# Reciprocal roots as a power on GpSimd, and another order of the first experts' splits and of the output norm, in a hybrid decoder trunk

## The chip, the cores and the metric

The kernel runs on one core of one Trainium2 chip. The metric is the device time of one execution in microseconds (us), as the median of several runs; a separate execution was profiled. The engines are TensorE (PE, with its weight loads PEld), VectorE (DVE), ScalarE (ACT), GpSimd (POOL) and SyncE (SP). SP issues most DMAs; POOL issues the indirect ones (gathers and scatters by token index). Each engine works through its own instructions in order.

## The reference

The input is 1024 tokens of 1024 channels and a memory of 256 tokens. One layer is computed in float32, then a last norm:

```
h = rmsnorm(x, g_mix); x = x + gated_branch_mixer(h)       # conv 31, pool, short conv, gates
x = x + cross_attention(rmsnorm(x, g_x), rmsnorm(mem, g_mem))
t = rmsnorm(x, g_ffn)
p_grp = softmax(t @ w_rg + b_rg); pick 1 of 4 groups
p_exp = softmax of the 4 experts in the group; pick 2, weights renormalized, times the group's
x = x + sum over the 2 experts of weight * (silu(t @ w_gate) * (t @ w_up)) @ w_down
out = rmsnorm(x, g_f)
rmsnorm(x, g) = x * (mean(x * x) + 1e-6) ** -0.5 * g
```

Sixteen experts of width 256. Every norm needs, for each token, the reciprocal root of its mean square; the change is about how that root is computed and where the last norm's work stands.

## The kernel before, in words

**Layout.** Tokens lie on the 128 partitions, so there are 8 row tiles of 128 tokens x 1024 channels. Matrix products are done in three float32r passes: each operand is split into a high part (`wh`, a cast on ScalarE) and a remainder (`wl`, a subtraction on VectorE or GpSimd, line 117), and `mm3` (lines 60 to 64) multiplies high by high, high by low and low by high. `Stream` loads weights into raw buffers (`load_to`, line 93) and splits them (`split_to`, lines 112 to 117) ahead of their use; `units_of` says which engines split an item. For the experts' stream, item `EW + 6 e + q` is block q (4 of gate and up, 2 of down) of expert e in the order of work.

**Order.** The order of the instructions on every engine is that of the program (a manual schedule): the mixer's projections, then row-tile loops "w" (output projection), "s" (scores) and "v" (attention output), with helpers for the next tile's work put between the matmuls, then the experts.

**Roots.** `rstd_of` (line 166) turns sums of squares, which ScalarE accumulates with a Square activation, into reciprocal roots: `v = ss / D + eps` (line 174), a first guess by integer shift and subtraction (lines 175 and 176), `v = -v / 2` (line 177), and three Newton rounds of two instructions for one column (lines 180 and 181) or four for several (lines 183 to 186). The first three are always on VectorE, the rest on `unit`: VectorE, or GpSimd for the mixer's input norm (two roots of 4 columns, `prep_rstd`), for the last norm's tiles, and for one of the final blocks. It is called for the memory (2 columns), the mixer's input, the 8 row tiles of the norm ahead of attention (`w_norm`), the 8 ahead of the experts (`post_v`, and by hand for the last tile) and the last norm.

**The last row tile before routing** (from line 1067). Row tile 7 of "v" is done in halves. `add_half` adds the residual on VectorE (line 1080), squares on ScalarE (line 1081), and multiplies by the gain on GpSimd (line 1082). The root scales the normalized row (line 1107, stored for the gathers by a DMA from ScalarE's queue) and the logits of routing (line 897), from which the experts, ranks and token lists of all slots follow; then the first gathers go out (line 1153).

**The first experts.** After the gathers of experts 0 and 1 the weights 4 and 5 are split (`ast.split_to(EW + 6)`); VectorE works out the weights of the slots, TensorE transposes expert 0's rows (line 1182) and sums the slot weights (`pw`, line 1235), weight 6 is split, gate-up of expert 0 (line 1197) runs, `wslot` is written (lines 1243 to 1245), and weights 7 to 9 are split. GpSimd takes the remainders of weights 4, 5 and 7.

**The experts.** Each expert e has up to two blocks of 128 slots. Block 0: gate-up (`gu`), Silu times up (`act_of`, lines 1255 and 1256), transposes (`at`, line 1291), `down` (`y`); block 1 (`xb`, `gub`, `atb`, `yb`) runs under an If on the count of tokens. The results of experts 0 to 13 are scaled by the slot weight and scatter-added to `x2` in DRAM (line 1157).

**The last norm.** While experts 14 and 15 (`E1`, `E2`) compute, all 8 row tiles of `x2` are loaded (`norm_load`, line 1324), squared (1328), scaled (1336) and stored to `out` (1337), as if the last two experts had added nothing. Their tokens' rows are gathered (`rows_in`), get the expert's result (`final_add`, line 1351), squares (1352), a root (`final_rstd`, line 1354) and scaling (1361), and are scattered over the rows in `out` (`rows_out`, line 1345). The scatters write the same tensor as the stores and as one another, so each waits until those before it have landed. The dictionary `HOOKS` (line 1383) says at which place of which expert each of these steps is issued; expert 15 is (-1, ...). In this input expert 14 has one block, expert 15 two, and three scatters are issued: (E1, 0), (E2, 0), (E2, 1).

## Time and profile before

| what | value |
|---|---|
| runs | 1354.13 us median of 3 (1353.12 to 1354.61) |
| profiled execution | 1349.84 us |
| its span, first to last instruction | 1348.2 us |
| mean granted TensorE clock | 0.974 of full speed |
| busy: PE, DVE, ACT, POOL | 1268.7, 811.1, 447.6, 144.9 us |

Times in rows are in us from the span's start unless marked ns. `x8` is the number of instructions merged in a row; the bracket at a row's end is the idle time of the engine just before it and what released it. `SPq` and `POOLq` are the instruction queues of SP and POOL (DMA issue, waits), L1337 is line 1337 of the kernel. Busy shares are averages over stages with different limits; the waits and the chain say what ended last at a place.

### The profile page before, as it was taken

To read this page: it belongs to the slowest core of one execution; us is meant where nothing else is said; L and a number is where in the kernel's file an instruction comes from. 1 tells how busy PE (TensorE), PEld (TensorE's weight loads), DVE (VectorE), ACT (ScalarE), POOL (GpSimd) and SP (SyncE) were. 2 spreads that over 40 slices of the span, in tenths; PEclk is the share of its full clock that TensorE was granted. 3 is DMA by queue.
4 is the path that set the end of the run, shared out by engine and by line. 5 is a ranking of instruction groups with operands and counts; after the bars stand their busy time and mean duration, and the time that the engine had idled before them with its cause. 6 is when DMAs were issued, how large, how long until landed. Compare 5 with 4: busy or idle time off the path is not lost. (4 is left out here: it accounts for less than half of the span.)

```text
span 1348.2 us, 16066 instructions
## 1 busy us (share of the span) xinstructions
PE 1268.7 (94%) x6150; PEld 1054.2 (78%) x6151; DVE 811.1 (60%) x1210; ACT 447.6 (33%) x611; POOL 144.9 (11%) x157
## 2 busy tenths in 40 slices
PE   7999999999999999999999999999999689998871
PEld 7988888888888888888888898887888477776661
DVE  5836787887874356322344554335777767657665
ACT  6511221221111133212132253435312456555571
POOL 2400000000000000000000020011000423212243
PEclk8999999999999999999999999999999799999986
DMA  7641111121111112111153240113434788979773
GB/s 290 214 145 47 39 63 32 52 78 33 50 58 48 48 34 60 42 52 63 32 199 114 94 158 2 57 43 121 137 113 159 259 285 272 271 216 343 243 240 144
DMA packets 46490, 166.83 MB, mean 124 GB/s; under 512 B 5376, under 2 KB 6144, under 8 KB 46400
## 3 DMA queue, kind: packets, MB, share of 16 engines
q1 hardware_dynamic: 40032, 142.84, 30.8%
q0 software_dynamic: 6224, 22.29, 6.8%
q8 instruction: 54, 0.88, 0.3%
q10 hardware_dynamic: 144, 0.52, 0.1%
q14 instruction: 36, 0.29, 0.1%
HBM read 134.70 MB, written 30.93 MB: 123 GB/s over the span
## 5 line engine op out<-in xcount | busy, mean ns | idle before, releaser
L117 DVE TENSOR_TENSOR wl<-raw,wh 128x1024 fp32r<-128x1024 f32 (+1 forms) x179 | 213.5, 1228 | 145.7 <-ACT wh L114 145.6
L60 PE MATMUL ps<-hTh,wh 128*128 128x512 f32 x768 | 238.1, 390 | 0.0
L64 PE MATMUL ps<-hTh,wl 128*128 128x512 f32 x768 | 237.8, 389 | 0.0
L62 PE MATMUL ps<-hTl,wh 128*128 128x512 f32 x768 | 237.8, 389 | 0.0
L114 ACT CAST wh<-raw 128x1024 fp32r<-128x1024 f32 x197 | 194.8, 1036 | 97.0 <-PE ps L62 42.2
L60 PEld LDWEIGHTS ps<-hTh,wh 128*128 128x128 f32 x768 | 144.1, 188 | 30.4 <-issue 0.5
L64 PEld LDWEIGHTS ps<-hTh,wl 128*128 128x128 f32 x768 | 144.0, 188 | 30.2 <-DVE wl L117 0.2
L62 PEld LDWEIGHTS ps<-hTl,wh 128*128 128x128 f32 x768 | 144.1, 188 | 29.9
L431 DVE SCALAR_TENSOR_TENSOR conv<-glu,colt,conv 128x1024 f32<-128x1024 f32 x120 | 154.1, 1284 | 3.5
L117 POOL TENSOR_TENSOR wl<-raw,wh 128x1024 fp32r<-128x1024 f32 x18 | 44.2, 2461 | 235.3 <-ACT wh L114 235.3
L1157 POOL DMA_INDIRECT x_d<-merged,toki x20 | 37.9, 1897 | 154.2 <-DVE merged L1304 72.2
L60 PE MATMUL v<-Bh,aht 128*128 128x512 f32 x128 | 43.5, 411 | 0.0
L62 PE MATMUL v<-Bl,aht 128*128 128x512 f32 x128 | 41.0, 391 | 0.0
L64 PE MATMUL v<-Bh,alt 128*128 128x512 f32 x128 | 41.0, 391 | 0.0
L60 PE MATMUL s<-Ah,aht 128*128 128x512 f32 x128 | 40.1, 394 | 0.1
L60 PE MATMUL w<-wh,aht 128*128 128x512 f32 x128 | 40.0, 394 | 0.0
L64 PE MATMUL w<-wh,alt 128*128 128x512 f32 x128 | 39.6, 390 | 0.5 <-DVE alt L202 0.5
L64 PE MATMUL s<-Ah,alt 128*128 128x512 f32 x128 | 39.5, 390 | 0.0
L62 PE MATMUL s<-Al,aht 128*128 128x512 f32 x128 | 39.5, 389 | 0.0
L62 PE MATMUL w<-wl,aht 128*128 128x512 f32 x128 | 39.4, 389 | 0.0
L1197 PE MATMUL gu<-wh,xh 128*128 128x512 f32 x120 | 35.1, 415 | 4.0 <-DVE aTl L202 2.1
L1182 PE MATMUL xe<-ident,merged 128*128 128x128 f32 x128 | 18.9, 294 | 18.8 <-DMA merged<-t_d,toki 15.0
(434 smaller groups left out, 2136.0 us busy)
## 6 DMA issues: line engine op xcount, KB each, us to landing
raw<-in_w_e_dram SPq DMA_DIRECT2D x93, 512.0 KB
raw<-in_w_in_dram SPq DMA_DIRECT2D x48, 512.0 KB
raw<-in_w_kv_dram SPq DMA_DIRECT2D x16, 512.0 KB
x_d<-res SPq DMA_DIRECT2D x16, 512.0 KB
xr<-in_x_dram SPq DMA_DIRECT2D x8, 512.0 KB
raw<-in_w_ac_dram SPq DMA_DIRECT2D x8, 512.0 KB
raw<-in_w_o_dram SPq DMA_DIRECT2D x8, 512.0 KB
res<-in_x_dram SPq DMA_DIRECT2D x8, 512.0 KB
```

The costliest lines, as they stand in the source:

```text
L60: nc.tensor.matmul(o, lhsT=lhs.hi, rhs=r.hi, start=first, stop=False)
L62: nc.tensor.matmul(o, lhsT=lhs.hi, rhs=r.lo, start=False, stop=False)
L64: nc.tensor.matmul(o, lhsT=lhs.lo, rhs=r.hi, start=False, stop=last)
L114: e_hi.copy(hi, raw)
L117: e_lo.tensor_tensor(lo, raw, hi.bitcast(F32), op=OP.subtract)
L431: fillers.append(lambda k=k: dve.scalar_tensor_tensor(conv[i], glu[:, k:k + S], col("conv_w", i * TAPS + k), conv[i], op0=OP.mult, op1=OP. ...
L1157: pool_e.indirect_dma_start(out=x2_d[:, :], out_offset=bass.IndirectOffsetOnAxis(ap=idx, axis=0), in_=ys, in_offset=None, compute_op=OP.add)
L1182: pe.transpose(ps[k // 4][:, k % 4 * P:(k % 4 + 1) * P], src[:, k * P:(k + 1) * P], ident)
L1197: pe.matmul(ps, lhsT=getattr(xs[h], x)[:, k, :], rhs=getattr(w[2 * h + k // 2], y)[:, c0:c0 + 512], start=(h, k, x, y) == (0, 0, "hi", "hi ...
```

## The change

`rstd_of` becomes two GpSimd instructions: a multiply-add and a power with an exponent of -0.5 from a constant tile, which one memset fills at the start. All roots go there, with any number of columns; there is no Newton round left on any engine. For row tile 7 of "v" the first half's sum goes through a multiply-add on GpSimd as well, and the second half's product with the gain goes to VectorE. The split of weights 4 and 5 moves behind the slot-weight arithmetic, that of weight 6 behind `wslot`, which is now written ahead of gate-up of expert 0; the splits up to weight 9 and the loads stand ahead of gate-up. In the last norm the squares of the tiles move out of the end of expert 14 into expert 15, in pairs with a root each; the squares of the final blocks become a step of their own (`final_squares`), and the roots of expert 15's two blocks stand ahead of the second scatter on POOL.

```diff
--- before.py
+++ after.py
@@ -147,6 +147,8 @@
     sm = psums.enter_context(tc.tile_pool(name="sm", bufs=2, space=PSUM))
     small = ctx.enter_context(tc.tile_pool(name="small", bufs=2))
 
+    minus_half = small.tile([P, 2 * NT], F32, tag="mh", bufs=1, name="minus_half")
+
     def acc_tile(name):
         t = acc.tile([P, D], F32, tag="acc", name=name)
         return t
@@ -163,27 +165,13 @@
         c = CW[name] + i
         return colt[:, c:c + 1]
 
-    def rstd_of(ss, name, n=1, unit=None, y=None, base=EPS):
-        unit = unit or dve
+    def rstd_of(ss, name, n=1, y=None, base=EPS):
         pool = small if y is None else mo
         v = pool.tile([P, NT], F32, tag="v", bufs=2, name=f"v_{name}")[:, :n]
-        q = pool.tile([P, NT], F32, tag="q", bufs=2, name=f"q_{name}")[:, :n]
         if y is None:
             y = pool.tile([P, NT], F32, tag="y", bufs=2, name=f"y_{name}")[:, :n]
-        yi = y.bitcast(I32)
-        dve.tensor_scalar(v, ss, 1.0 / D, base, op0=OP.mult, op1=OP.add)
-        dve.tensor_scalar(yi, v.bitcast(I32), 1, None, op0=OP.logical_shift_right)
-        dve.tensor_scalar(yi, yi, -1, 0x5F3759DF, op0=OP.mult, op1=OP.add)
-        unit.tensor_scalar(v, v, -0.5, None, op0=OP.mult)
-        for _ in range(3):
-            if n == 1:
-                unit.tensor_scalar(q, y, v, y, op0=OP.mult, op1=OP.mult)
-                unit.tensor_scalar(y, q, 1.5, y, op0=OP.add, op1=OP.mult)
-            else:
-                unit.tensor_tensor(q, y, v, op=OP.mult)
-                unit.tensor_tensor(q, q, y, op=OP.mult)
-                unit.tensor_scalar(q, q, 1.5, None, op0=OP.add)
-                unit.tensor_tensor(y, q, y, op=OP.mult)
+        pool_e.tensor_scalar(v, ss, 1.0 / D, base, op0=OP.mult, op1=OP.add)
+        pool_e.tensor_tensor(y, v, minus_half[:, :n], op=OP.pow)
         return y
 
     def sumsq(src, junk, name):
@@ -238,6 +226,7 @@
     make_identity(nc, ident)
     dve.memset(onesm, 1.0 / 512)
     dve.memset(epst, EPS)
+    pool_e.memset(minus_half, -0.5)
     st.load_to(3)
     x_load(0)
     x_load(1)
@@ -255,7 +244,7 @@
         act.activation(junk, xr[key], AF.Square, accum_out=sums[b][:, i:i + 1])
 
     def prep_rstd(b, n):
-        rstds[b] = rstd_of(sums[b], b, n, unit=dve if b == "m" else pool_e)
+        rstds[b] = rstd_of(sums[b], b, n)
 
     def prep_scale(key, b, i, g):
         xn = pp.tile([P, D], F32, tag="xn", bufs=2, name=f"xn_{key}")
@@ -1079,7 +1068,7 @@
     def add_half(h):
         dve.tensor_tensor(x2[:, cols(h)], ph[h], x2[:, cols(h)], op=OP.add)
         act.activation(xn[:, cols(h)], x2[:, cols(h)], AF.Square, accum_out=(ss, ss2)[h])
-        pool_e.tensor_tensor(xgr[:, cols(h)], x2[:, cols(h)], grow[:, cols(h)], op=OP.mult)
+        (dve if h else pool_e).tensor_tensor(xgr[:, cols(h)], x2[:, cols(h)], grow[:, cols(h)], op=OP.mult)
 
     def tr_half(h):
         if not h:
@@ -1098,7 +1087,7 @@
     ast.load_to(EW + 2 * T7)
     add_half(1)
     nc.sync.dma_start(x2_d[T7 * P:, :][0:P, :], x2)
-    dve.tensor_scalar(ss, ss, 1.0 / D, EPS, op0=OP.mult, op1=OP.add)
+    pool_e.tensor_scalar(ss, ss, 1.0 / D, EPS, op0=OP.mult, op1=OP.add)
     rstd7 = rstd_of(ss2, "v7", base=ss)
     rt7 = sm.tile([P, 512], F32, tag="sm", name="rt7")
     logits(rt7, tT7, range(4))
@@ -1175,7 +1164,6 @@
 
     gather_both(0)
     gather_both(1)
-    ast.split_to(EW + 6)
 
     def x_tr(src, ps):
         for k in range(KD):
@@ -1219,6 +1207,7 @@
         dve.tensor_copy(wpart[:, :, :, c, :], wfull)
         if c < 2:
             dve.tensor_tensor(wfull, wfull, wpart[:, :, :, c, :], op=OP.subtract)
+    ast.split_to(EW + 6)
     xp = act_split("x0")
     xs0 = [xp[:, 4 * h:4 * h + 4, :] for h in range(2)]
     pxe = [acc_tile(f"xe0_{h}")[:, 0:512] for h in range(2)]
@@ -1236,13 +1225,14 @@
                           rhs=wpart[:, k, t].rearrange("p c e -> p (c e)"),
                           start=k == 0 and t == 0, stop=k == 1 and t == NT - 1)
     x_split(pxe, xs0)
-    ast.split_to(EW + 7)
-    w = [ast.get(EW + q) for q in range(6)]
-    gu0 = gate_up(xs0, w, acc_tile("gu0")[:, 0:512])
     pw3 = pw[:, 0:6 * NE].rearrange("p (b c e) -> p b c e", b=2, c=3)
     dve.tensor_copy(wslot, pw3[:, :, 0, :])
     dve.tensor_tensor(wslot, wslot, pw3[:, :, 1, :], op=OP.add)
     dve.tensor_tensor(wslot, wslot, pw3[:, :, 2, :], op=OP.add)
+    ast.split_to(EW + 10)
+    ast.load_to(EW + 18)
+    w = [ast.get(EW + q) for q in range(6)]
+    gu0 = gate_up(xs0, w, acc_tile("gu0")[:, 0:512])
     att.close()
     mo = ctx.enter_context(tc.tile_pool(name="mo", bufs=1, reuse_waits="tile"))
 
@@ -1257,10 +1247,11 @@
         return sg
 
     def gate_up_out(e, ps):
-        ast.split_to(EW + 6 * e + (8 if e else 10))
-        ast.load_to(EW + 6 * e + 23)
         if e == 0:
             gather_both(2)
+            return act_of(ps, f"{e}")
+        ast.split_to(EW + 6 * e + 8)
+        ast.load_to(EW + 6 * e + 23)
         return act_of(ps, f"{e}")
 
     def next_in(e, ps):
@@ -1268,6 +1259,7 @@
         x_in(xg[e + 1, 0], ps, xs)
         return xs
 
+    ast.load_to(EW + 23)
     sg = gate_up_out(0, gu0)
     xs1 = xs_tile("0b")
     xs0 = next_in(0, [sm.tile([P, 512], F32, tag="sm", name=f"xe1_{h}") for h in range(2)])
@@ -1328,7 +1320,7 @@
             act.activation(fjunk, nat[t], AF.Square, accum_out=nsum[:, t:t + 1])
 
     def norm_rstd(t0, t1):
-        rstd_of(nsum[:, t0:t1], f"n{t0}", t1 - t0, pool_e, nrstd[:, t0:t1])
+        rstd_of(nsum[:, t0:t1], f"n{t0}", t1 - t0, nrstd[:, t0:t1])
 
     def norm_scale(*ts):
         for t in ts:
@@ -1349,12 +1341,16 @@
         for h in range(2):
             f = fin[e, b][:, h * 512:(h + 1) * 512]
             dve.scalar_tensor_tensor(f, ps[h], w_of_slot(e, b), f, op0=OP.mult, op1=OP.add)
+
+    def final_squares(e, b):
+        for h in range(2):
+            f = fin[e, b][:, h * 512:(h + 1) * 512]
             act.activation(fjunk[:, 0:512], f, AF.Square, accum_out=fsum[:, e - NF, b, h:h + 1])
 
-    def final_rstd(e, b, unit):
+    def final_rstd(e, b):
         ss = fsum[:, e - NF, b]
-        dve.tensor_tensor(ss[:, 0:1], ss[:, 0:1], ss[:, 1:2], op=OP.add)
-        rstd_of(ss[:, 0:1], f"f{e}_{b}", 1, unit, frstd[:, e - NF, b:b + 1])
+        pool_e.tensor_scalar(ss[:, 0:1], ss[:, 0:1], 1.0 / D, EPS, op0=OP.mult, op1=OP.add)
+        rstd_of(ss[:, 1:2], f"f{e}_{b}", 1, frstd[:, e - NF, b:b + 1], base=ss[:, 0:1])
 
     def final_scale(e, b):
         f = fin[e, b]
@@ -1366,7 +1362,8 @@
         else:
             final_add(ps, e, b)
             if b and e < E2:
-                final_rstd(e, b, dve)
+                final_squares(e, b)
+                final_rstd(e, b)
                 final_scale(e, b)
 
     E1, E2 = NF, NE - 1
@@ -1381,12 +1378,13 @@
         rows_out(out, E1, 0)
 
     HOOKS = {
-        (-2, "end"): [lambda: norm_squares(0, 1, 2, 3), lambda: rows_in(E2, 0), lambda: norm_rstd(0, 4)],
-        (-1, "act"): [lambda: norm_squares(4)],
-        (-1, "put"): [lambda: norm_squares(5, 6, 7), lambda: norm_scale(0, 1, 2), lambda: norm_rstd(4, 8), lambda: norm_scale(3)],
-        (-1, "gate"): [lambda: final_rstd(E1, 0, pool_e)],
-        (-1, "act1"): [lambda: norm_scale(4, 5, 6, 7), lambda: final_scale(E1, 0), first_rows_out],
-        (-1, "put0"): [lambda: final_rstd(E2, 0, dve)],
+        (-2, "end"): [lambda: rows_in(E2, 0)],
+        (-1, "act"): [lambda: norm_squares(0, 1), lambda: norm_rstd(0, 2), lambda: norm_squares(2, 3), lambda: norm_rstd(2, 4)],
+        (-1, "put"): [lambda: norm_scale(0, 1, 2), lambda: norm_squares(4)],
+        (-1, "gate"): [lambda: norm_squares(5), lambda: norm_rstd(4, 6), lambda: norm_scale(3), lambda: norm_squares(6)],
+        (-1, "act1"): [lambda: norm_squares(7), lambda: norm_rstd(6, 8), lambda: final_squares(E1, 0), lambda: final_rstd(E1, 0),
+                       lambda: norm_scale(4, 5, 6, 7), lambda: final_scale(E1, 0), first_rows_out],
+        (-1, "put0"): [lambda: final_squares(E2, 0), lambda: final_rstd(E2, 0)],
         (-1, "late"): [lambda: final_scale(E2, 0), lambda: rows_out(out, E2, 0)],
     }
 
@@ -1445,8 +1443,9 @@
             down(yp1, aT1, w, 1)
             put(yp1, e, 1)
             if end:
+                final_squares(e, 1)
+                final_rstd(e, 1)
                 hook(e, "late")
-                final_rstd(e, 1, dve)
                 final_scale(e, 1)
                 rows_out(out, e, 1)
         with cmp.Else():
```

## Rows read from the trace of the kernel before

**Rows 1.** The page, busy time, share of the span and instructions of TensorE.

```profile
PE 1268.7 (94%) x6150; PEld 1054.2 (78%) x6151; DVE 811.1 (60%) x1210; ACT 447.6 (33%) x611; POOL 144.9 (11%) x157
```

**Rows 2.** Waits of TensorE over the span: in total, times, longest (us).

```profile
PE xe L1182 <- DMA merged<-t_d,toki: 15.0, 6, 4.4
```

**Rows 3.** Timeline of the start: start us, us, engine, line, operation, [idle].

```profile
42.44 0.23 POOL L177 TENSOR_SCALAR v<-v 128x4 f32<-128x4 f32 x1 [0.32 <-DVE y L175]
...
45.01 1.22 DVE L117 TENSOR_TENSOR wl<-raw,wh 128x1024 fp32r<-128x1024 f32 x1
...
47.11 2.39 POOL L117 TENSOR_TENSOR wl<-raw,wh 128x1024 fp32r<-128x1024 f32 x1
...
47.19 3.39 DVE L262 SCALAR_TENSOR_TENSOR xn<-xr,y,g_mix 128x1024 f32<-128x1024 f32 x1 [0.96 <-POOL y L186]
...
50.73 1.06 PE L197 MATMUL tr<-ident,xn 128*128 128x128 f32 x8 [1.27 <-DVE xn L262]
```

**Rows 4.** Timeline around the last row tile before routing.

```profile
1043.02 1.27 POOL L1082 TENSOR_TENSOR merged<-res,grow 128x512 f32<-128x512 f32 x1 [2.75 <-DVE ss_v7a L1101]
...
1043.57 0.19 ACT L1081 ACTIVATION_READ_ACCUMULATOR xnv<-res 128x1 f32 x1
...
1044.33 1.07 PE L889 MATMUL rt<-w_rt,merged 128*128 128x20 f32 x8 [0.49 <-ACT merged L1089]
...
1046.23 0.24 DVE L897 SCALAR_TENSOR_TENSOR lg<-rt,y_v,b_rt 128x20 f32<-128x20 f32 x1
```

**Rows 5.** Timeline around the first experts.

```profile
1057.87 7.12 POOL L117 TENSOR_TENSOR wl<-raw,wh 128x1024 fp32r<-128x1024 f32 x3
...
1059.99 6.09 DVE L117 TENSOR_TENSOR wl<-raw,wh 128x1024 fp32r<-128x1024 f32 x1
...
1066.01 0.18 DVE L1243 COPY wslot<-pw 128x32 f32<-128x32 f32 x1
...
1066.78 0.63 PE L1182 MATMUL xe<-ident,merged 128*128 128x128 f32 x4 [1.64 <-DVE wslot L1245]
...
1070.58 0.66 PE L1291 MATMUL at<-ident,sg 128*128 128x128 f32 x2 [3.17 <-DVE xl L202]
```

**Rows 6.** Timeline of the last expert.

```profile
1300.69 1.07 PE L1197 MATMUL gu<-wh,xl 128*128 128x512 f32 x4
...
1305.54 0.36 ACT L1255 ACTIVATE sg<-gu 128x256 f32<-128x256 f32 x1
...
1306.71 0.41 PE L1291 MATMUL at<-ident,sg 128*128 128x128 f32 x2 [3.37 <-DVE sg L1256]
...
1314.86 0.23 POOL L177 TENSOR_SCALAR v_n<-v_n 128x4 f32<-128x4 f32 x1 [1.64 <-DVE nrstd L175]
...
1318.03 0.42 DVE L202 TENSOR_TENSOR aTlb<-atb,aThb 128x256 fp32r<-128x256 f32 x1 [0.90 <-ACT aThb L201]
...
1319.41 4.89 DVE L1336 SCALAR_TENSOR_TENSOR nat<-nat,nrstd,grow 128x1024 f32<-128x1024 f32 x4 [0.96 <-POOL nrstd L186]
```

**Rows 7.** The same timeline, small instructions of GpSimd.

```profile
1306.13 0.24 POOL L177 TENSOR_SCALAR v_n<-v_n 128x4 f32<-128x4 f32 x1 [6.16 <-DVE nrstd L175]
...
1306.45 0.20 POOL L183 TENSOR_TENSOR q_n<-nrstd,v_n 128x4 f32<-128x4 f32 x1
...
1319.67 2.27 POOL L180 TENSOR_SCALAR q_f<-frstd,v_f 128x1 f32<-128x1 f32 x1
...
1325.42 0.27 POOL L181 TENSOR_SCALAR frstd<-q_f,frstd 128x1 f32<-128x1 f32 x1
```

**Rows 8.** The chain of waits at the end: start us, us, what.

```profile
1327.86 0.08 POOLq L1379
...
1329.17 3.45 DMA out_dram<-merged,toki
...
1334.50 3.33 DMA out_dram<-merged,toki
...
1338.59 0.90 POOL out_dram L1345
```

## The prediction

> **What bounds the kernel now.** I read the page first, then TensorE's waits, then the timeline around the places that the diff touches, and last the chain of waits. On the page the reader is to see that TensorE is busy for 94% of the span [rows 1]: an edit pays only where TensorE stands still, or behind its last matmul. The list of TensorE's waits says where it stands still [rows 2]: mostly behind gathers of tokens, which the diff leaves alone, and once, near 50 us, behind a normalized row tile, which needs a root [rows 3]. The four timelines that follow are the places touched: the start [rows 3], the last row tile before routing [rows 4], the first experts [rows 5] and the last expert with the output norm [rows 6]. The chain shows the end of the span, where TensorE has nothing left to do: three scatters into the output, one behind the other [rows 8].
>
> **Price of a root.** Before, a root is four instructions and three Newton rounds; after, it is a multiply-add and a power, both on GpSimd (the final ones two multiply-adds and a power). GpSimd's small multiply-add takes 0.24 us, a small product of two tiles 0.20 us, one with a scalar from a tile 0.27 us, and about 0.08 us lie between two of them [rows 7]. The trace has no power. Ends: 0.2 us, as the plain product, and 2.4 us, which GpSimd takes for a difference over 1024 columns [rows 3]; a function in place of a product on so few columns should lie near the small row, and I take **0.6 us** (an estimate: three times that row). A root is then 0.24 + 0.08 + 0.6 = 0.9 us, a final one 0.9 + 0.35 = 1.3 us.
>
> **The start.** GpSimd's root of row tiles 4 to 7 works from 42.44 until the weight remainder queued behind it starts at 47.11; VectorE's scaling of tile 4, in the same two microseconds, takes 3.39 us, and TensorE waits 1.27 us for it [rows 3]. With the root done by 43.4 the remainder moves some 2.5 us ahead, still next to VectorE's own remainder (45.01), which may then wait until about 47.0; scaling follows at 48.2 and ends at 49.5, where TensorE came free (50.73 - 1.27 = 49.46). I take **-1.0 us**; ends 0 and -1.3. The memory's root, that of tiles 0 to 3, the 8 of the next norm and the first 7 of the third go at nothing: their users are transposes and logits behind the matmuls of the following tile, and no other wait of TensorE names a root; VectorE's freed time lies under TensorE's matmuls too. GpSimd's weight remainders stand ahead of at most one such root, 2.4 us [rows 3]; without that cover it would be this much per root. The added memset of 16 columns lies ahead of GpSimd's first remainder, which waits for a weight.
>
> **The last row tile before routing.** ScalarE's sum of the second half is there at 1043.76, VectorE's ten instructions follow, and the logits' scaling on VectorE starts at 1046.23, while TensorE's last logits were done at 1044.33 + 1.07 = 1045.40 [rows 4]. After: GpSimd, idle for the 2.75 us before 1043.02 [rows 4], has its first multiply-add behind it; the second starts at 1043.85, and 0.27 + 0.08 + 0.6 put the root at 1044.8. The logits come last now: 1045.5, **-0.7 us**, until a power of 1.2 us. The second half's product with the gain (1.27 us on GpSimd [rows 4]) goes to VectorE, which has the 2.4 us of its root free there. The row's store leaves earlier too; the gather waits for the slots, not for it.
>
> **The first experts.** VectorE's remainder of weight 6 stands from 1059.99 to 1066.08, released only when GpSimd's three remainders end at 1064.99; the slot weights follow, and then two remainders [rows 5]. After, the three slot instructions (from 1066.01, some 0.2 us each) come first, at a time when VectorE would stand still anyway: **-0.6 us** for TensorE's transposes at 1070.58, which wait 3.17 us for the end of this queue. The second half of the next expert's transposes loses its wait of 1.64 us [rows 5], but the queue named ends last, so no more is counted. The splits of weights 4 and 5 move behind three small activations on ScalarE; GpSimd takes them only after its gathers at 1057.87, so nothing, and if ScalarE were late, the lateness. SP issues the same loads in the same order, POOL the same gathers.
>
> **The last expert.** gate-up ends at 1301.76, but ScalarE's Silu starts at 1305.54, behind squares of four row tiles that wait for their loads, and the transposes wait 3.37 us, until 1306.71 [rows 6]. After, Silu precedes the squares: the transposes go when the three matmuls ahead of them end, near 1303.3, **3.4 us** earlier, and all that follows on TensorE with them. VectorE's remainder of the second block (1318.03 to 1318.45) ends near 1315.05. Then come the last four scalings, which start at 1319.41 now since GpSimd's second Newton (from 1314.86) holds them [rows 6]. After, the pairs' roots are ready except the last: tile 7's square follows ScalarE's cast, some 3.4 us earlier too, at 1314.6 to 1315.85, the multiply-add is held by two scalings until 1317.7, the power ends at 1318.4. Scalings 4 and 5 from 1315.1, 6 and 7 from 1318.5 to 1320.95, against 1324.30: **-3.3 us** for the last store. The gather of expert 15's second block now stands ahead of the roots on POOL, not between them.
>
> **The scatters.** The first waits until POOL's queue moves on at 1327.86, when the stores have landed, and starts 1.31 us later; the second starts 5.33 us after it, the third 4.09 us after that [rows 8]. Landing takes 3.45 us, and from landing to the next start the third shows 0.76 us, so 4.2 us is the least. The 5.33 contain VectorE's Newton, sum and scaling. After, the roots of expert 15 stand on POOL behind the first scatter, the new wait: 0.9 us for issuing a scatter [rows 8], two roots of 1.3 us, and 0.8 us of gaps and semaphores, as from landing to start, give 4.3 us: **-1.0 us**. The final roots queue ahead of the second scatter, and whoever waits for them is VectorE's scaling and, through it, the third scatter, which keeps its 4.1 us.
>
> **Sum.** -1.0 - 0.7 - 0.6 - 3.3 - 1.0 = **-6.6 us**. The profiled execution took 1349.84 us (1348.2 of them its span), so 1343.2; it lies 4.3 us under the median of the runs, from which I take the same: **1347.5 us**. A power of 0.2 us gives 0.7 us more (1346.8). From 1.2 us on each further microsecond costs four: one before routing, one ahead of the last stores, two between scatters. With power c the change is 4c - 9.6, so 2.4 us gives 0 and 1354.1.
>
> **A rule weighed.** VectorE's stream of scalings holds GpSimd: the first scalar product takes 2.27 us next to it and one of the same kind after its end 0.27 us [rows 7]. The Trainium skill (SBUF — State Buffer, section Who interferes with whom) has it that a VectorE instruction with two inputs in SBUF and a GpSimd instruction that reads SBUF exclude each other, and that who issues first keeps the port for the whole instruction. By that rule the last pair's multiply-add waits for one scaling, and the sum gains some 0.2 us; the row shows that two can pass, which I used.
>
> **Rivals.**
> - *A slow power* (the other side). It sits in the queue of POOL between the scatters, twice, and before routing, once. For it: the trace has no such instruction, and VectorE's Newton, 1043.76 to 1046.23, was cheap [rows 4]. Against: the small rows there lie under 0.3 us when undisturbed [rows 7]. From 3.1 us it is slower by more than 0.2%; at 4 us, 4 x 4 - 9.6 = +6.4, **1360.5**. Chance 0.07; a power of 1.7 to 3.1 us, within 0.2%, 0.05.
> - *The experts swallow what comes before them.* For it: TensorE waits 15.0 us for gathers there [rows 2], which share DMA with the weights. Against: gathers and loads are released by work that itself comes earlier. Then only the tail's 4.3 us are left: **1349.8**. Chance 0.10.
> - *The port lock holds the paired roots.* Four roots of two instructions are strewn among eight scalings; at 2.27 us each instruction the last pairs come some 4 us later, the gain ahead of the stores goes, and about 2.6 us remain: **1351.5**. Against: VectorE stops when a root is missing, and then GpSimd runs. Chance 0.08.
> - *Forecast:* 0.70.
>
> **Numbers.** A measurement here can tell about 0.2% (2.7 us). Faster: 0.70 + 0.10 = 0.80; same: 0.08 + 0.05 = 0.13; slower 0.07. The range goes from 1344.8 (power 0.2 us, the whole 1.64 us of the transposes' wait, and the runs' spread of 0.8 us) to 1352.0, over the two rivals that are faster or even; what is left out is the slow power and a little below.
>
> **What would show it.** Each power near 0.6 us on GpSimd; no wait of TensorE's transposes near 49.5; the logits' scaling bound by TensorE; slot weights ahead of the remainder; Silu of expert 15 right behind gate-up; the last store some 3 us sooner against the experts' end; scatters 4.3 and 4.1 us apart. It is wrong if the power takes over 1.2 us, if the roots between the scatters set their distance, or if the last expert starts as late as before.

## The result and the profile after

The runs gave 1342.74 us for the kernel after (median of 5, 1339.88 to 1345.01) and 1354.13 us for the kernel before (median of 5, 1351.45 to 1356.98): a ratio of **0.9921 [0.9900, 0.9942]**, or -11.4 us between the medians. Predicted were 1347.5 us (range 1344.8 to 1352.0) and -6.6 us. The direction was right, the time lies below the range. The profiled execution after took 1344.64 us, with a span of 1342.9 us, so the two profiles differ by only 5.3 us of span. Which of these numbers is the change's is the first question that the experiments answer. Two executions of the kernel before beside later runs took 2587 and 3282 us; they are in no number here.

The page after, its line of busy times, answers to [rows 1]: TensorE has the same work, VectorE has lost 41 us and 214 instructions, most of them of the Newton rounds.

```profile
PE 1268.5 (94%) x6150; PEld 1055.0 (79%) x6151; DVE 770.4 (57%) x996; ACT 447.2 (33%) x611; POOL 147.1 (11%) x154
```

The start, in the timeline of after, answers to [rows 3] (start us, us, engine, line, operation, idle time before it).

```profile
40.55 1.01 POOL L174 TENSOR_TENSOR y<-v,minus_half 128x4 f32<-128x4 f32 x1
...
42.87 2.42 POOL L117 TENSOR_TENSOR wl<-raw,wh 128x1024 fp32r<-128x1024 f32 x1 [1.31 <-ACT wh L114]
43.20 3.16 DVE L117 TENSOR_TENSOR wl<-raw,wh 128x1024 fp32r<-128x1024 f32 x1
...
46.42 0.39 PE L64 MATMUL kv<-memTh,wl 128*128 128x256 f32 x1 [1.07 <-DVE wl L117]
```

A power of four columns takes 1.01 us. TensorE no longer waits for the scaled row tile. GpSimd's remainder now runs against VectorE's instead (43.20: 3.16 us for what takes 1.2 alone), and TensorE waits 1.07 us for that.

Row tile 7 and the first gather, same view, answer to [rows 4].

```profile
1041.69 0.27 POOL L173 TENSOR_SCALAR v_v<-ss_v7b,ss_v7a 128x1 f32<-128x1 f32 x1 [3.36 <-ACT xnv L1070]
1042.04 0.55 POOL L174 TENSOR_TENSOR y_v<-v_v,minus_half 128x1 f32<-128x1 f32 x1
1042.08 1.07 PE L878 MATMUL rt<-w_rt,merged 128*128 128x20 f32 x8 [0.49 <-ACT merged L1078]
...
1043.27 0.24 DVE L886 SCALAR_TENSOR_TENSOR lg<-rt,y_v,b_rt 128x20 f32<-128x20 f32 x1 [1.45 <-PE rk L904]
...
1043.80 0.35 ACTq L1097 DMA_DIRECT2D t_d<-xnv  x1
...
1049.21 0.19 DVE L933 TENSOR_TENSOR toki<-idxf,pi 128x32 int32<-128x32 f32 x1 [0.40 <-PE pc L1109]
...
1050.77 1.24 POOL L1142 DMA_INDIRECT merged<-t_d,toki  x1 [8.19 <-DVE gv L1201]
```

One column takes 0.55 us, and the logits' scaling (1043.27) now stands right behind TensorE's last logits (1042.08 + 1.07), as forecast. But the gather starts 1.56 us behind the token list (`toki`). In the profile that the prediction read it was 0.49 us:

```profile
1047.41 0.35 ACTq L1108 DMA_DIRECT2D t_d<-xnv  x1
...
1052.17 0.19 DVE L944 TENSOR_TENSOR toki<-idxf,pi 128x32 int32<-128x32 f32 x1 [0.40 <-PE pc L1120]
...
1052.66 1.21 POOL L1153 DMA_INDIRECT merged<-t_d,toki  x1 [8.37 <-DVE cntf L1167]
```

The first experts answer to [rows 5].

```profile
1055.50 7.09 POOL L117 TENSOR_TENSOR wl<-raw,wh 128x1024 fp32r<-128x1024 f32 x3
...
1058.65 0.19 DVE L1229 COPY wslot<-pw 128x32 f32<-128x32 f32 x1
...
1059.20 4.48 DVE L117 TENSOR_TENSOR wl<-raw,wh 128x1024 fp32r<-128x1024 f32 x1
...
1067.63 0.41 PE L1283 MATMUL at<-ident,sg 128*128 128x128 f32 x2 [2.55 <-DVE xl L190]
```

The last expert and the scatters answer to [rows 6 to 8].

```profile
1300.58 0.39 ACT L1245 ACTIVATE sg<-gu 128x256 f32<-128x256 f32 x1 [4.95 <-PE gu L1185]
...
1301.94 0.38 PE L1283 MATMUL at<-ident,sg 128*128 128x128 f32 x2
...
1306.10 2.48 DVE L1328 SCALAR_TENSOR_TENSOR nat<-nat,nrstd,grow 128x1024 f32<-128x1024 f32 x2 [0.90 <-POOL nrstd L174]
...
1307.42 1.21 POOL L173 TENSOR_SCALAR v_n<-nsum 128x2 f32<-128x2 f32 x1 [1.36 <-ACT fjunk L1320]
...
1316.63 2.48 DVE L1328 SCALAR_TENSOR_TENSOR nat<-nat,nrstd,grow 128x1024 f32<-128x1024 f32 x2 [0.58 <-POOL nrstd L174]
1316.68 1.28 POOL L1352 TENSOR_SCALAR fsum<-fsum 128x1 f32<-128x1 f32 x1
...
1319.33 0.56 POOL L174 TENSOR_TENSOR frstd<-v_f,minus_half 128x1 f32<-128x1 f32 x1
...
1322.84 1.07 POOL L1337 DMA_INDIRECT out_dram<-merged,toki  x1 [2.95 <-DVE merged L1343]
...
1325.27 1.28 POOL L1352 TENSOR_SCALAR fsum<-fsum 128x1 f32<-128x1 f32 x1
...
1327.59 1.28 DVE L1357 SCALAR_TENSOR_TENSOR merged<-merged,frstd,grow 128x1024 f32<-128x1024 f32 x1 [1.08 <-POOL frstd L174]
1327.74 2.07 POOL L1337 DMA_INDIRECT out_dram<-merged,toki  x1 [0.19 <-issue]
1333.36 0.90 POOL L1337 DMA_INDIRECT out_dram<-merged,toki  x1 [3.55 <-DMA out_dram<-merged,toki]
```

Silu stands right behind gate-up and the transposes wait for nothing. The scatters are 4.90 and 5.62 us apart, where 4.3 and 4.1 were forecast: the issue of the second one took 2.07 us next to a scaling on VectorE (1.07 us for the first), and the third waits for its landing.

### The profile page after: what moved, and what is told of

It is laid out like the page before. It is cut to its first block, busy times and chain, and to the rows that moved or that the text cites. A ratio compares the mean times of both kernels' runs of the same rounds, so it can differ in the third digit from the quotient of the medians.

```text
span 1342.9 us, 15878 instructions
## 1 busy us (share of the span) xinstructions
PE 1268.5 (94%) x6150; PEld 1055.0 (79%) x6151; DVE 770.4 (57%) x996; ACT 447.2 (33%) x611; POOL 147.1 (11%) x154
## 5 line engine op out<-in xcount | busy, mean ns | idle before, releaser
L117 DVE TENSOR_TENSOR wl<-raw,wh 128x1024 fp32r<-128x1024 f32 (+1 forms) x179 | 213.9, 1230 | 152.9 <-ACT wh L114 152.8
L1146 POOL DMA_INDIRECT x_d<-merged,toki x20 | 34.9, 1745 | 158.8 <-DVE merged L1296 57.1
L190 DVE TENSOR_TENSOR alt<-merged,aht 128x1024 fp32r<-128x1024 f32 (+1 forms) x25 | 30.4, 1221 | 13.1 <-ACT aht L189 13.1
```

The lines of the kernel that those rows point to most:

```text
L117: e_lo.tensor_tensor(lo, raw, hi.bitcast(F32), op=OP.subtract)
L190: dve.tensor_tensor(dst.lo, src, dst.hi.bitcast(F32), op=OP.subtract)
L1146: pool_e.indirect_dma_start(out=x2_d[:, :], out_offset=bass.IndirectOffsetOnAxis(ap=idx, axis=0), in_=ys, in_offset=None, compute_op=OP.add)
```

## The experiments

A term is small beside the differences between executions, so each experiment is read twice: in its ratio, and in the time between landmarks of its trace.

**The two kernels again.** No edit.

> The kernel before, unchanged, to see how far its executions lie apart and in what. Theory A (the profiled execution of before was a fast draw): single times spread over some 7 us, the median stays near 1353 to 1354, and the ratio to before is 1.000; the trace of a slow draw shows its extra microseconds in the experts' stage, as more time at the lower granted clock or longer waits for gathers. Theory B (the two profiles are typical and the change is worth the 5.2 us between them): executions lie within 1 us of 1350 when they share a chip with the others of this group.

Measured: 1352.85 us (1350.39 to 1359.17, 12 runs), ratio 0.9997 [0.9981, 1.0014], span 1353.4 us.

> The changed kernel, unchanged, beside the one before on one chip. Theory A: ratio 0.990 to 0.994 (10 us less), although the two profiles differ by 5.2 us alone. Theory B: ratio 0.996 (5 us less).

Measured: 1344.81 us (1343.09 to 1347.72, 6 runs), ratio 0.9937 [0.9919, 0.9955], span 1346.1 us.

> The kernel after, unchanged. Theory A (true change about -9 us, the mean over its executions so far): ratio 0.9925 to 0.994. Theory B (the -6.6 us of the prediction was right and the first sets were draws): ratio 0.995.

Measured, on another chip: 1343.59 us (1342.52 to 1345.38, 6 runs), ratio 0.9924 [0.9906, 0.9943], span 1341.3 us.

Theory A holds in the times; where a long execution loses its time is looked at below. All executions of before, 86 of them, have a mean of 1353.1 us and a standard deviation of 2.4; the profiled one, 1349.84, has 7 below it. The 17 executions of after have a mean of 1343.9. The change is worth **-9.1 us**, with some 0.5 us for the standard error of the two means.

**Parts of the change.** First the roots alone, with the experts' order and the norm's order of before:

```diff
-        dve.tensor_scalar(v, ss, 1.0 / D, base, op0=OP.mult, op1=OP.add)
...
-                unit.tensor_tensor(y, q, y, op=OP.mult)
+        pool_e.tensor_scalar(v, ss, 1.0 / D, base, op0=OP.mult, op1=OP.add)
+        pool_e.tensor_tensor(y, v, minus_half[:, :n], op=OP.pow)
```

> All roots by power on GpSimd, and row tile 7's sum and product as in the change, but the first experts and the last norm in the order of before. By the steps of the prediction and the trace of after: start -1.6, later row tiles -0.7, routing -0.7, and in the last norm GpSimd's second root takes 1.9 instead of 4.5 us and the final roots no longer hold VectorE, -2 to -4: -5 to -7 us in all (ratio 0.995 to 0.996). Rival: nearly the whole gain is in the roots, then -9 us or more (ratio under 0.9935); other rival: without the new order of the squares the tail gains nothing, then -3 us (0.998).

Measured: 1349.48 us (1344.9 to 1352.9, 11 runs), ratio 0.9970 [0.9954, 0.9987]; -4.2 us between the means. The end of the kernel did not gain (from the first load of the norm's rows to the third scatter 43.2 us, before 43.0 and 44.3).

Then the kernel after without the change's second part (splits, loads and `wslot` stand as before):

```diff
     x_split(pxe, xs0)
+    ast.split_to(EW + 7)
+    w = [ast.get(EW + q) for q in range(6)]
+    gu0 = gate_up(xs0, w, acc_tile("gu0")[:, 0:512])
     pw3 = pw[:, 0:6 * NE].rearrange("p (b c e) -> p b c e", b=2, c=3)
...
-    ast.split_to(EW + 10)
-    ast.load_to(EW + 18)
-    w = [ast.get(EW + q) for q in range(6)]
-    gu0 = gate_up(xs0, w, acc_tile("gu0")[:, 0:512])
...
```

> The change without its second part: splits 4 to 6 and the slot weights as before, roots and last norm as after. By the prediction's step the part is worth 0.6 us: time as after within 1 us, at most 1 us more. Rival (the experts' order carries what the prediction missed, by keeping TensorE's clock or by earlier gathers): 3 us or more above after.

Measured: 1342.83 us (1339.81 to 1345.99, 6 runs), ratio 0.9924 [0.9904, 0.9944]. It is not slower than after on the same chip (1344.81), so the rival falls. And the same part alone, on the kernel before (the diff of the change, from `ast.split_to(EW + 6)` to `ast.load_to(EW + 23)`):

> The kernel before with the second part of the change alone (splits 6 to 10 and the slot weights in the other order), Newton roots and the last norm as before. Theory A (the prediction's term, and what the profiles with and without it show at that place): first expert's first transposes to its gated products' transposes 12.2 to 12.6 us in place of 12.8 to 13.3, total -0.6 us, ratio 0.9985 to 1.001, not to be told from no change. Theory B (the later splits and loads cost something further on, as the 1 us between the kernels with and without this part suggests): ratio 1.0005 to 1.002.

Measured: 1353.74 us (1351.32 to 1356.70, 12 runs), ratio 1.0005 [0.9991, 1.0020]. From the token list to expert 0's `at` transposes it takes 17.83 us where four profiles with the old order and Newton roots show 18.4: -0.57 us at its place, nothing that can be told in the total. Theory A.

Then the last norm. Only the first four squares behind Silu, all roots by Newton:

```diff
-        (-2, "end"): [lambda: norm_squares(0, 1, 2, 3), lambda: rows_in(E2, 0), lambda: norm_rstd(0, 4)],
-        (-1, "act"): [lambda: norm_squares(4)],
+        (-2, "end"): [lambda: rows_in(E2, 0)],
+        (-1, "act"): [lambda: norm_squares(0, 1, 2, 3), lambda: norm_rstd(0, 4), lambda: norm_squares(4)],
```

> The kernel before with one thing of the last norm moved: the squares of row tiles 0 to 3 and their root stand behind the last expert's Silu, roots by Newton's steps as before. Theory A (the step of the prediction, 3.4 us on PE): the wait of the last expert's transposes for the gated products (3.4 to 4.9 us before) falls under 1 us, the last scatter lies 2 to 3.4 us earlier counted from the first load of the norm's rows (43.0 and 44.3 in the two profiles of before, so 40 to 42), ratio 0.9975 to 0.9985. Theory B (PE gains it, but the Newton root of the four tiles now comes late and the scalings wait for it): same short PE wait, but the scatters stand where they stood, ratio 0.9995 to 1.0005.

Measured: 1353.71 us (1349.00 to 1356.77, 12 runs), ratio 1.0003 [0.9988, 1.0018]. Theory B, to the letter; the timeline of this kernel shows it.

```profile
1306.10 0.39 ACT L1255 ACTIVATE sg<-gu 128x256 f32<-128x256 f32 x1 [5.17 <-PE gu L1197]
...
1307.49 0.38 PE L1291 MATMUL at<-ident,sg 128*128 128x128 f32 x2
...
1317.13 3.68 DVE L1336 SCALAR_TENSOR_TENSOR nat<-nat,nrstd,grow 128x1024 f32<-128x1024 f32 x3 [2.28 <-POOL nrstd L186]
...
1326.31 4.89 DVE L1336 SCALAR_TENSOR_TENSOR nat<-nat,nrstd,grow 128x1024 f32<-128x1024 f32 x4 [1.33 <-POOL nrstd L186]
```

The transposes wait for nothing, as in after. The scalings wait for Newton's steps on GpSimd, and the third scatter comes 44.1 us behind the first load of the norm's rows, as before.

The whole new order on the kernel before, with its Newton roots; `HOOKS` and `final_squares` are those of after but for the engine of expert 15's roots, 12 Newton instructions and one product a pair on GpSimd:

```diff
-        (-1, "act"): [lambda: norm_squares(4)],
+        (-1, "act"): [lambda: norm_squares(0, 1), lambda: norm_rstd(0, 2), lambda: norm_squares(2, 3), lambda: norm_rstd(2, 4)],
...
-        (-1, "put0"): [lambda: final_rstd(E2, 0, dve)],
+        (-1, "put0"): [lambda: final_squares(E2, 0), lambda: final_rstd(E2, 0, dve)],
```

> The whole new order of the last norm, with Newton's steps in all roots (pairs on GpSimd, 14 small instructions each). Theory A (order and power belong together): four Newton roots of about 3 us each on GpSimd stand ahead of the scalings of the last tiles, the last scaling ends 2 to 5 us later than with the power, and with the 3.4 us that PE gains the sum is -2 to +2 us, ratio 0.9985 to 1.0015. Theory B (the order carries all of the end's gain, the power nothing): -5 us, ratio 0.996.

Measured: 1360.28 us (1358.21 to 1362.20, 6 runs), ratio 1.0061 [1.0040, 1.0081]. Slower than both theories: the order by itself costs 7.6 us between the means. In this kernel's timeline:

```profile
1321.20 1.11 POOL L183 TENSOR_TENSOR q_n<-nrstd,v_n 128x2 f32<-128x2 f32 x1
...
1326.40 2.49 DVE L1336 SCALAR_TENSOR_TENSOR nat<-nat,nrstd,grow 128x1024 f32<-128x1024 f32 x2 [2.95 <-POOL nrstd L186]
1326.66 2.28 POOL L180 TENSOR_SCALAR q_f<-frstd,v_f 128x1 f32<-128x1 f32 x1
...
1334.08 1.07 POOL L1345 DMA_INDIRECT out_dram<-merged,toki  x1 [3.14 <-DVE merged L1351]
1343.16 1.76 POOL L1345 DMA_INDIRECT out_dram<-merged,toki  x1 [8.01 <-DVE merged L1365]
1349.08 0.90 POOL L1345 DMA_INDIRECT out_dram<-merged,toki  x1 [4.16 <-DMA out_dram<-merged,toki]
```

The last pair's scalings wait 2.95 us for their root, and both of expert 15's Newton roots, on VectorE here, lie between the first two scatters, which are 9.08 us apart. So neither the power (roots alone) nor the order (this kernel) gains anything at the end; together they gain 3.6 us.

**The gather's new wait.** The store of row tile 7 is moved ahead of two weight loads:

```diff
-    ast.load_to(EW + 2 * T7)
     add_half(1)
...
-    act.dma_start(t_d[T7 * P:S, :], xn)
+    nc.sync.dma_start(t_d[T7 * P:S, :], xn)
+    ast.load_to(EW + 2 * T7)
```

> The kernel after, with the store of the last row tile's normalized rows on SP's queue ahead of the two expert weight loads that stand before it now. Theory A (the first gather waits for that store's landing, which shares the DMA engines with the 1 MB of weights issued just before it): the first gather starts 0.5 to 0.9 us behind the slots' tokens (1.6 in the profiles of after), the first expert's transposes 0.7 to 1.1 us earlier, ratio 0.9925 to 0.993. Theory B (the gather waits for something else, counts or GpSimd's own queue): the gap stays 1.5 to 1.6 us, ratio 0.993 to 0.995. The loads now go 2 to 4 us later; if the first expert's casts wait for them, that shows as a DMA wait on ScalarE and gives the gain back.

Measured: 1344.95 us (1340.55 to 1350.48, 10 runs), ratio 0.9954 [0.9934, 0.9974]. In this kernel's timeline:

```profile
1049.36 0.19 DVE L933 TENSOR_TENSOR toki<-idxf,pi 128x32 int32<-128x32 f32 x1 [0.40 <-PE pc L1109]
...
1049.86 1.24 POOL L1142 DMA_INDIRECT merged<-t_d,toki  x1 [7.11 <-DVE cntf L1156]
...
1055.08 7.11 POOL L117 TENSOR_TENSOR wl<-raw,wh 128x1024 fp32r<-128x1024 f32 x3
...
1057.45 5.84 DVE L117 TENSOR_TENSOR wl<-raw,wh 128x1024 fp32r<-128x1024 f32 x1
...
1067.23 0.66 PE L1283 MATMUL at<-ident,sg 128*128 128x128 f32 x2 [4.51 <-DVE xl L190]
```

The mechanism is theory A's: with the store ahead of the 1 MB of weights the gather starts 0.50 us behind the token list. The traces also have the store's landing: in the 14 other profiles, with powers or Newton roots, the gather starts 0.88 or 0.89 us behind it. In after the store is issued 3.0 to 3.5 us behind the two loads and lands 6.1 us later, at 1049.88. In the profile of before it was issued 4.4 to 4.9 us behind them and landed 4.4 us later, at 1051.78. Here it goes ahead of them and lands 3.1 us later, at 1047.07, before the token list is there. The experiment also moves the store from ScalarE's queue to SP's, and does not tell the queue from the order; before and after have the same queue. Of the 1.1 us won there 0.57 reach the `at` transposes (17.87 us behind the token list instead of 18.44). The second and third gather move by less, so GpSimd's three remainders start 5.72 us behind the token list where after has 6.29, and VectorE's remainder (5.84 us) is held until they end. In the total nothing is won that can be seen.

**A better end.** The second scatter's scaling and issue go ahead of the last slots' root, as they were before the change:

```diff
             if end:
+                hook(e, "late")
                 final_squares(e, 1)
                 final_rstd(e, 1)
-                hook(e, "late")
```

> The kernel after, with the second scatter's scaling and issue ahead of the last slots' squares and root, as they stood before. Theory A (the power roots and the descriptors of the second scatter are held by VectorE's scalings next to them, which is what stretched the step from second to third scatter to 5.6 us): first to second 4.3 to 4.5, second to third 4.1 to 4.4, so 8.5 to 8.9 in place of 10.5, ratio 0.9920 beside 0.9934 for the two runs of after. Theory B (the third scatter waits for the landing of the second anyway, whichever order): first to third stays 10 to 10.5, ratio 0.993 to 0.994.

Measured: 1340.18 us (1337.72 to 1344.53, 6 runs), ratio 0.9919 [0.9896, 0.9942].

> Once more the kernel after with the second scatter's scaling and issue ahead of the last slots' root, beside after itself on the same chip. Theory A: 1.5 to 2 us under after, first to third scatter 8.5 to 8.9 us; ratio 0.991 to 0.9925. Theory B (the lower median of its first set was a draw): within 0.5 us of after.

Measured: 1343.42 us (1338.82 to 1346.50, 6 runs), ratio 0.9913 [0.9889, 0.9936]; after_again on the same chip 1343.59, so the gain is not seen between these two medians. The trace shows it in both profiles, 8.65 and 8.71 us from first to third scatter against 10.5; here the timeline of the first of the two.

```profile
1318.76 1.07 POOL L1337 DMA_INDIRECT out_dram<-merged,toki  x1 [2.98 <-DVE merged L1343]
...
1323.21 1.06 POOL L1337 DMA_INDIRECT out_dram<-merged,toki  x1 [2.09 <-DVE merged L1357]
...
1327.41 0.98 POOL L1337 DMA_INDIRECT out_dram<-merged,toki  x1 [1.86 <-DVE merged L1357]
```

The issue of the second scatter takes 1.06 us again, with no scaling beside it. Then the last tile of the norm was also scaled and stored in two halves:

```diff
-            dve.scalar_tensor_tensor(nat[t], nat[t], r, grow2, op0=OP.mult, op1=OP.mult)
-            nc.sync.dma_start(out[t * P:(t + 1) * P, :], nat[t])
+            for c in ([slice(0, 512), slice(512, D)] if t == NT - 1 else [slice(0, D)]):
+                dve.scalar_tensor_tensor(nat[t][:, c], nat[t][:, c], r, grow2[:, c], op0=OP.mult, op1=OP.mult)
+                nc.sync.dma_start(out[t * P:(t + 1) * P, c], nat[t][:, c])
```

> The kernel with the early second scatter, and the last tile of the norm scaled and stored in two halves. Theory A (the first scatter waits for the landing of the last tile's store, 3.7 us behind its scaling): the last half store is smaller and lands earlier, last scaling to first scatter 3.0 to 3.3 us, 0.3 to 0.7 us off the total, ratio 0.9905 to 0.9925. Theory B (the first scatter waits for the scaling of its own rows): the gap stays 3.7 to 3.8 us and nothing is gained.

Measured: 1339.69 us (1338.80 to 1346.51, 6 runs), ratio 0.9900 [0.9878, 0.9922]; from the last scaling to the first scatter 3.58 us against 3.76 and 3.81, in a second profile 4.73. The halves win nothing that holds. The 24 executions with the early second scatter, with the halves and without (halves_again, below, among them), have a mean of 1341.7 us against 1343.9 for after: it is worth about 2 us, and these are the fastest forms of the kernel here.

**What makes executions differ.** Behind the first experts, up to the norm's first load, the same code took 211.9 to 218.8 us over 15 profiles. In five of them TensorE waited 4.6 to 5.1 us once for weight casts near 1230 us (mean 217.5 us for the stretch), in the other ten at most 2.5 (mean 214.4). The waits of TensorE and of ScalarE in two profiles of before, each row from the list of its engine. First the profile that the prediction read:

```profile
PE gu L1197 <- ACT wh L114: 1.7, 1, 1.7
...
ACT merged L1306 <- DMA x_d<-merged,toki: 3.7, 1, 3.7
```

And the kernel before in its second profile:

```profile
PE gu L1197 <- ACT wh L114: 4.8, 1, 4.8
...
ACT merged L1306 <- DMA x_d<-merged,toki: 6.8, 1, 6.8
```

ScalarE's write of a weighted output waits for the scatter that last used its buffer, and the casts queue behind it. To take that wait away, a fourth output buffer was taken from the gathered rows. With four buffers the rows of some second blocks are overwritten by a gather for a later expert before they are used, so these two kernels compute those blocks from other rows.

```diff
-    SLOTS = {"x": (3, 4, 5, 6, 7), "y": (0, 1, 2), "f": (0, 1, 2, 5)}
+    SLOTS = {"x": (4, 5, 6, 7), "y": (0, 1, 2, 3), "f": (0, 1, 2, 5)}
```

> The kernel late_halves with four buffers for the experts' weighted outputs in place of three, and four for the gathered rows in place of five. Theory A (executions of one kernel spread over 7 us because near 1230 us ScalarE's write of an output waits 1.8 to 7.1 us for the landing of the scatter that last used the buffer, and PE then waits up to 5.1 us for weight casts): that DMA wait on ScalarE is gone, PE's wait for casts is under 2.2 us, gub0 to the norm's first load 212 to 214 us, the spread of the executions under 4 us, ratio 0.989 to 0.990. Theory B (gathered rows now come late with one buffer fewer, or the casts are late for another reason): PE's wait for gathered rows over the 12 to 14 us of the other profiles, ratio above 0.992.

Measured: 1382.79 us (1375.68 to 1383.92, 6 runs), ratio 1.0202 [1.0177, 1.0226].

> The kernel before with the same exchange of buffers. Theory A: ratio 0.997 to 0.9985 and a spread under 4 us, its profile within 1 us of its median. Theory B: ratio 1.000 or above, spread 7 us as before.

Measured: 1386.87 us (1385.96 to 1389.85, 5 runs), ratio 1.0260 [1.0240, 1.0280].

> The kernel late_halves again, unchanged, beside the two on one chip. Theory A: two groups of executions some 6 us apart again (near 1339.5 and 1346), ratio 0.990 to 0.992. Theory B: one group, the two of the first set were chance.

Measured: 1342.37 us (1339.21 to 1343.72, 6 runs), ratio 0.9921 [0.9903, 0.9938]; no two groups 6 us apart. The exchange was a miss: TensorE's second blocks now wait for gathers, and ScalarE waits for scatters six times, 34.8 us in all, so it says nothing about the one wait. That this wait makes executions differ is borne out by its place in the longer profiles, and not shown by an experiment: two profiles with short waits (roots_only and silu_first) took 217.0 and 218.6 us there as well.

The granted clock accounts for these two as well. Over the same 15 profiles TensorE spent 13.0 to 26.5 us of this stretch at the lower level of its clock, and the stretch is longer by 0.6 us for each of them (correlation 0.89; with the wait for casts 0.59). Roots_only has 20.9 us at the lower level, silu_first 26.5. The stretch as a window in silu_first and in late_first, which has 13.0 us (us, busy time of PE, PEld, DVE, ACT and POOL with instructions, granted clock, DMA share, GB/s):

```profile
1082.77:1301.37 218.60, 194.73 (x884) 156.22 (x883) 144.45 (x179) 125.04 (x178) 56.67 (x37) 0.94 0.82 258
...
1076.92:1289.25 212.33, 187.75 (x880) 150.66 (x879) 141.84 (x177) 122.31 (x176) 55.42 (x37) 0.97 0.86 270
```

TensorE is busy 7.0 us longer with the same work in a stretch that is 6.3 us longer. The whole executions agree: of the kernel before, 81 with their clock on record have a correlation of -0.64 between time and mean granted clock. That the clock makes most of the differences is read from these numbers and no experiment set it; what brings the lower level at one time and not at another stays open.

## Why the prediction was right or wrong

The table compares the prediction's terms with the mean over all profiles in which the code of a stretch is that of before (5; at the end the 2 of the kernel before itself) or of after (10; from the token list to `at` 4 and 7, at the end the 3 of the kernel after itself). Stretches are measured between starts of instructions.

| stretch | predicted | before | after | change |
|---|---|---|---|---|
| start to the mixer's first matmul (`ps`) | -1.0 | 70.2 | 68.3 | -1.9 |
| from there to the last loop (other roots) | 0 | 862.9 | 862.3 | -0.6 |
| last loop to row tile 7's logits | -0.7 | 114.36 | 113.68 | -0.7 |
| token list to expert 0's `at` | -0.6 | 18.40 | 18.44 | 0 |
| from there to its second block | 0 | 10.3 | 9.1 | -1.3 |
| second block to the norm's first load | 0 | 214.9 | 215.7 | not told apart |
| norm's first load to the third scatter | -4.3 | 43.7 | 40.0 | -3.6 |

The changes add up to -8.1 us, and the runs say -9.1 with 0.5 of error; the prediction said -6.6. The row of the end hangs on few profiles: the end of experts_order_only has the code of before and shows 46.3, those of no_experts_order and store_first have the code of after and show 39.9 and 39.8. With them the change is -4.6.

**Price of a root: right.** 0.55 us for one column against 0.6; it is some 0.7 for two and 1.01 for four, which was not foreseen and did no harm that shows. The rival of the slow power falls with this row.

**The start: right in kind, too small.** The step "I take -1.0 us; ends 0 and -1.3" rested on one wait of 1.27 us in one execution. In the five profiles with Newton roots TensorE waits 1.3, 2.7, 1.8, 2.2 and 3.4 us for scaled row tiles between 20 and 72 us, in four of them twice; in the ten with powers never, but 0 to 1.6 us for the remainder that GpSimd now holds. The wait of the row, near 50 us, is 1.1 to 1.5 us in all five. The other one, of 0.7 to 1.9 us near 30 us, is missing only in the profile that the prediction read. So the step that failed is "that of tiles 0 to 3 ... go at nothing". In same_before the first scaling waits 2.71 us on VectorE for GpSimd's Newton rounds, and TensorE for the scaling:

```profile
28.54 1.28 DVE L262 SCALAR_TENSOR_TENSOR xn<-xr,y,g_mix 128x1024 f32<-128x1024 f32 x1 [2.71 <-POOL y L186]
...
29.96 1.07 PE L197 MATMUL tr<-ident,xn 128*128 128x128 f32 x8 [1.38 <-DVE xn L262]
```

In the profile of before VectorE waited as long (2.69 us), but TensorE had work left: that the row held one wait and not two was chance.

**All other roots at nothing: wrong by 0.6 us.** The loops that follow the mixer are bound by TensorE, and the step argued that freed VectorE time lies under its matmuls. The loop "w" got 0.46 us shorter (117.9 in all ten profiles with powers, 118.3 or 118.4 in the five without), the way from "s" to the last loop 0.13 us in the mean. In "w" the loss lay at the loop's end: in before the last row tile's Newton rounds stand on VectorE ahead of its scaling and of the remainder `Al`, and the first matmul of "s" waits for `Al`. It starts 0.46 us later behind the loop's start than in after; the row's first transpose starts only 0.06 us later.

**Row tile 7: right**, term and mechanism. **"The gather waits for the slots, not for it": wrong.** It waits for the landing of the row's store, as store_first and the landings show, and in before it did so too: it starts 0.49 us behind the token list in the profile read, where both came at the same time, and 0.70 to 0.87 us in the other four with Newton roots. The store leaves 3.6 us earlier than in the profile of before (1043.80 against 1047.41), but beside the two weight loads issued just ahead of it, and the gather that reads it starts only 1.9 us earlier (1050.77 against 1052.66). This costs 0.57 us at expert 0's transposes and cancels the term of the first experts, which is right by itself (-0.57 measured, -0.6 predicted).

**A term that was not in the sum.** Behind expert 0 the granted clock was at its lower level for a shorter time. Two windows of the same stretch, first of the kernel before in its second profile (us, busy time of PE, PEld, DVE, ACT and POOL with instructions, granted clock, DMA share, GB/s):

```profile
1070.00:1084.00 14.00, 11.84 (x50) 9.86 (x51) 9.55 (x14) 6.97 (x11) 2.10 (x2) 0.76 1.03 369
```

And of the kernel after in its second profile:

```profile
1070.00:1084.00 14.00, 14.00 (x73) 11.74 (x72) 8.33 (x12) 7.31 (x12) 2.28 (x2) 1.00 1.02 368
```

TensorE comes to this stretch from a wait of 2.1 to 4.5 us, and at 0.5 (1.2 GHz) four matmuls of 512 columns take 1.91 us (at 1074.33 in the first of these profiles) instead of 1.07 at full clock (2.4 GHz). In the 12 us ahead of the window it is the other way round, a granted clock of 1.00 in the first profile and 0.86 in the second: there the lower level fell into gate-up of expert 0, which waits for VectorE afterwards in any case. The stretch takes about 8.3, 9.9 or 11.1 us; none of the five profiles with Newton roots shows 8.3, six of the ten with powers do. store_first, with powers, shows 11.1, so this is a likelihood and no fixed gain.

**The end: right in its sum, wrong in its parts.** Counted from the norm's first load, the last scaling ends 3.6 us earlier (predicted 3.3). The first scatter follows it by 3.72 us instead of 4.87, not predicted: the prediction let it wait for the stores, but in before GpSimd's own queue came last there. Its last Newton instruction starts at 1325.42 [rows 7], 1.1 us behind the end of the last scaling, and the scatter 3.75 us later; the stores had landed by 1327.33, 1.0 us before the queue was through its waits. In after the last power starts at 1319.33, 0.2 us behind the end of the last scaling, the scatter 3.51 us later, and the last store lands when the queue comes to it (1321.96). First to second scatter takes 4.90 (predicted 4.3) because a sum on GpSimd is held by a scaling for 1.28 us; second to third takes 5.62, where "keeps its 4.1 us" failed: the scaling of the last rows now stands next to the second scatter's issue, which takes 2.07 us, and the scatter lands 4.86 us behind its start; without that neighbour (late_first) they are 1.06 and 3.43 us. late_first takes both losses back. The step also missed why the end gains at all: Silu's earlier start is worth 3.4 us on TensorE and nothing in the time (silu_first), unless the roots behind it are short.

**The rivals.** That the experts swallow what comes before them is half true: at expert 0's transposes the 0.6 us of its own order were eaten, while the start's gain came through. That the port lock holds the paired roots was seen and stayed small: three of the four paired roots lost 0.7 to 1.3 us to scalings, and the scalings waited 0.58 to 0.90 us for roots. The rule weighed in the prediction (the Trainium skill, SBUF — State Buffer, section Who interferes with whom) agrees with two rows of after: GpSimd's multiply-add at 1307.42 ends at 1308.63, when the scaling then running ends (1306.10 + 2.48 = 1308.58), and the one at 1316.68 ends at 1317.96, behind the first of the two scalings from 1316.63 on (1.24 us each) and not behind both. In norm_order_newton the product at 1326.66 takes 2.28 us beside two scalings, as in [rows 7]: there two pass. When one passes and when two is not shown.

**The baseline and the range.** To lay the change against the median of the runs and not against the profiled execution was right; that execution lay 3.2 us under the mean of 86. The time came out 4.8 us under the prediction: 2.5 from the change, 1.1 because the median given was that much above the mean of before, 1.2 because the five runs of after lay below the mean of 17. That last part is luck; without it the time, 1343.9, would still lie under the range. The steps of the prediction that failed are the terms put at nothing: the root of tiles 0 to 3, for which TensorE waited in four of five profiles (the start -1.9 us and not -1.0), and "all other roots", -0.6 us; the granted clock behind expert 0, -1.3 us on the mean, was in no term. The range was too narrow by "the runs' spread of 0.8 us", taken from three runs; the executions' standard deviation is 2.4 us. The three parts named for its lower end, taken off 1347.5, give 1344.4 and not 1344.8; the time lies under both.

## What to carry to other kernels

A wait of a microsecond in one profiled execution is a sample: two profiles of the same kernel, side by side, would have shown the start's waits at 1.3 and 2.7 us and the whole at 1348.2 and 1353.4. Where a reordering puts small GpSimd work between VectorE's long instructions, count how many instructions a result needs there: two per root made this order pay, thirteen made it cost 7.6 us. When a store leaves earlier, look at what else its queue and the DMA engines carry at that moment before its reader is counted as free of it.

## What the runs showed that was not expected

The issue of a scatter on GpSimd takes 1.06 to 1.07 us alone or next to VectorE's `final_add`, one of whose inputs is in PSUM, and 2.07 us next to a scaling with both inputs in SBUF, in the five profiles with the order of after (1.76 in norm_order_newton, where the scaling had started 0.36 us ahead and not 0.15); its landing goes from 3.43 to 4.86 us. A power on GpSimd depends on the columns (0.55, some 0.7 and 1.01 us for 1, 2 and 4), where a product of two tiles stays at 0.20 us for 2 and for 4. Executions of one kernel on one chip differ by 7 us and more, at mean granted clocks between 0.97 and 0.985, the longer ones mostly at the lower.
